# A hybrid decoder block on one core: seven Strassen gate pairs instead of six, operand sums from a stored x, early products in turn, and LayerNorm written behind the third pair

## The chip, the cores and the metric

The kernel runs on one core of one Trainium2 chip. The metric is the device time of one execution in microseconds (us); three executions of the kernel before gave 1420.69, 1419.81 and 1416.16 us, median 1419.81 us. The engines are named as in the profile: PE (TensorE), DVE (VectorE), ACT (ScalarE), POOL (GpSimd) and SP (SyncE, which here only issues DMAs). Each engine works through its own instructions in the order in which the compiled program has them.

## The reference, cut to what matters

One layer, sequence 1024, width 1024, everything float32:

```python
mod = silu(c) @ ada_w + ada_b
sh1, sc1, ga1, sh2, sc2, ga2 = split(mod, 6)
h = rmsnorm(x, pre_mix_g) * (1 + sc1) + sh1
glu_in, qkv, gates = split(h @ w_in, [1024, 2560])       # gates: 2 x 1024 columns
u = silu(layernorm(causal_depthwise_conv(glu(glu_in))))  # 512 channels
y_conv = u @ w_conv_out                                  # 512 -> 1024
y_att = stick_breaking_attention(qkv) @ w_att_out        # 512 -> 1024
g_conv, g_att = split(gates, 2)
y = (sigmoid(g_conv) * y_conv + sigmoid(g_att) * y_att) @ w_o
x = x + ga1 * rmsnorm(y, post_mix_g)
# then a SwiGLU sub-layer of the same build
```

The change concerns the product for `gates`, a 1024 x 2048 weight times h, the LayerNorm of the convolution branch, and the two stages behind them, `u @ w_conv_out` and `o @ w_att_out`.

## The kernel before, in words

Activations lie transposed: h is eight tiles of 128 channels x 1024 positions. Each float32 operand is split into two parts of the fp32r type, hi and lo (`hhi[k]`, `hlo[k]`), and a product takes three matmuls: hi by hi, hi by lo, lo by hi. A matmul instruction is 128x128 weights by 512 positions, into one bank of PSUM.

The stages stand in this order: the first RMSNorm and projections; attention, GLU and convolution; the gates; LayerNorm; `y_conv` (L772); `y_att` (L801 on); the product by w_o; the SwiGLU sub-layer. The order of instructions on each engine is made by a scheduler from the program order, the priorities in the code and the moment at which it thinks that data and buffers are free, so that pieces of later stages stand between earlier ones. A ring is a set of buffers with one tag: the n-th tile takes the buffer of the (n - bufs)-th and waits until that one's last reader is done.

**Gates.** The 16 row blocks of the gate matrix form eight pairs. `NPL` = 2 pairs (four blocks `n`) are plain products (L611-615, bank `pg`): 24 matmuls for each half of the positions, 192 in all. The other six pairs are 2x2 block products by a seven-product scheme of Strassen's kind: 7 products of 12 matmuls instead of 8. Two products of a pair, with the unchanged operands B11 (`hhi[0..3]`, `hlo[0..3]`) and B21 (`hhi[4..7]`, `hlo[4..7]`), are the early ones (L617-628): each has its own bank (`k1`, `k2`), the first is copied to `ee0` and stored to DRAM (`e_d0`), the second is added to it on DVE. 144 matmuls in all. The other five (`other_five`, L697-712) use the banks `ka` and `kc` and weight sums `s1`..`s4`: 360 matmuls in all. Their data operands T1..T4 are sums of blocks of h, formed once (L660-670): `f` is a ring of two tiles of 128x1024, filled on DVE with hi + lo, four subtractions follow for each `j`, and `make_t` splits each sum in hi (ACT) and lo (DVE).

**LayerNorm.** `ln_all` (L722-759) loads the convolution's result (`cr0`..`cr3`) and works in two halves of 512 positions: sums over channels by a matmul with ones (`lnm`, `lnv`), subtraction, squares, reciprocal root, then swish into `csil`, from which `chi` and `clo` are split. It is written behind the first pair (`LN_AT` = 0) with a raised priority (`LN_PRI` = 100). Its tiles come from the ring `hp` (tag `act`, 16 buffers), whose first 16 tiles are hhi and hlo, in turn.

**The two products behind.** `y_conv(n)` (L772-783) is 24 matmuls for each of eight `n`, into `pyc`; weights `wc0, 2, 4, 6` come through `load_w` by the ring `wraw` (three buffers of 128x1024 in the pool `wp`). Behind each `y_conv` stand two dots on DVE (`ada2_dots`, L764), by which the modulation of the second sub-layer is formed; their weights `ada2_16..31` come through the ring `f` (two buffers). Then `of0`..`of3` (the attention output, ring `wraw`) are split into `ohi`, `olo`, and `y_att` needs those and `wa0, 2, 4, 6` (ring `wraw` too) for `pya`.

Loads are issued by SP, one after another; an issue that waits for a buffer holds up those behind it. Stores to the DRAM tiles of the gates are issued by POOL.

Of the kernel before, what the change touches and what calls it, by code (L numbers as in the profile page):

```python
# [47 lines left out]
LN_AT = 0  # L48
SOONER = 5000
EARLY = 11  # L50
TLATER = 40
# [22 lines left out]
def tile_block(ctx: ExitStack, tc: tile.TileContext, xT, vecs, ada1, ada2, win, wv, wcv, wat, wo, w1, w2, cvw, out):  # L74
# [15 lines left out]
    cb_d = dp.tile([P, D], F32, name="cb_d")  # L90
    s_d = [dp.tile([P, T], F32, name=f"s_d{n}") for n in range(2 * KT)]
    e_d0 = [dp.tile([P, CH], F32, name=f"e_d0_{i}") for i in range(KT)]
    g_d = [dp.tile([P, 2, 2, CH], F32, name=f"g_d{k}") for k in range(FH)]
    w_d = [dp.tile([P, 4, 2, CH], F32, name=f"w_d{k}") for k in range(FH)]

# [5 lines left out]
    def load(dst, src):  # L101
        return nc.sync.dma_start(dst, src)
# [100 lines left out]
    with ExitStack() as s0:  # L203
# [146 lines left out]
        for k in range(KT):  # L350
            kn = k + 1
            if kn < KT:
                if kn not in SH_DVE:
                    shift_act(kn)
                if kn + 1 < KT and kn + 1 not in SH_DVE:
                    shift_pe(kn + 1)
                x_op(kn)
                if kn <= 2:
                    w0_hi(kn)
                hi_op(kn)  # L360
                if kn + 1 < KT:
                    dots(kn + 1)
                if kn <= 2:
                    w0_lo(kn)
            if k:
                lo_op(k)
            ws = (q0b, k0b, gg0b)
            if k <= 1:
                for i in range(k + 1):
                    gemm_k(ws[i], w0s[i], k)  # L370
                for kk in range(k + 1):
                    gemm_k(ws[k + 1], w0s[k + 1], kk)
            else:
                for b_, w_ in zip(ws, w0s):
                    gemm_k(b_, w_, k)
# [34 lines left out]
    with ExitStack() as sC:  # L410
        pc = mkpool(sC, "pc")
        with ExitStack() as sA:
# [196 lines left out]
            for n in PLAIN:  # L609
                gb = banks2(f"pg{n}")  # L610
                gemm(gb, load_w(win[20 + n], f"wg{n}"), h, range(KT))  # L611
                for c in range(NCH):
                    sg = sgp.tile([P, CH], F32, tag="sg", name=f"sg{n}_{c}", bufs=2)
                    act.activation(sg, gb[c], AF.Sigmoid, bias=0.0, scale=1.0)
                    store(s_d[n][:, c * CH:(c + 1) * CH], sg)
            for i in GPAIRS:
                raw = wp.tile([P, T], F32, tag="wraw", name=f"ew{i}")  # L617
                load(raw, win[20 + 2 * i])
# [3 lines left out]
                act.activation(e[0], k1, AF.Copy)  # L622
                store(e_d0[i], e[0])
# [3 lines left out]
                act.activation(e[1], e[1], AF.Sigmoid, bias=0.0, scale=1.0)  # L627
                store(s_d[2 * i][:, :CH], e[1])

    sV.close()  # L630
    with ExitStack() as sG:
# [22 lines left out]
        def make_t(name, src, hi_eng, lo_eng):  # L654
# [2 lines left out]
            lo_eng.tensor_tensor(t[:, 1], src, t[:, 0], op=ALU.subtract)  # L657
            return t

        for j in range(HK):  # L660
# [3 lines left out]
            b11, b12, b21, b22 = f[0][:, :CH], f[0][:, CH:], f[1][:, :CH], f[1][:, CH:]  # L664
            dve.tensor_tensor(b11, b12, b11, op=ALU.subtract)
            dve.tensor_tensor(b12, b22, b12, op=ALU.subtract)
            dve.tensor_tensor(b22, b22, b11, op=ALU.subtract)
            dve.tensor_tensor(b21, b21, b22, op=ALU.subtract)
            for b, src in (("T2", b22), ("T3", b12), ("T1", b11), ("T4", b21)):
                B0[b, j] = make_t(f"{b}o_{j}", src, act, dve)  # L670

        pairs, p1s = {}, {}
# [13 lines left out]

        def other_five(i):
            wg, wu = pairs[i]
            p1 = p1s[i]
            a11, a12, a21, a22 = wg[:, :CH], wg[:, CH:], wu[:, :CH], wu[:, CH:]  # L690
            s1, s2, s3 = (st(f"g{nm}_{i}") for nm in ("s1", "s2", "s3"))
            v, w_, c21 = xt(f"gv_{i}"), xt(f"gw_{i}"), xt(f"gc_{i}")
            dve.tensor_tensor(s1, a21, a22, op=ALU.add)
            dve.tensor_tensor(s2, s1, a11, op=ALU.subtract)
            s2o = w_op(f"s2o_{i}", s2, act, GP)
# [15 lines left out]
            dve.tensor_tensor(c21, ka, p1, op=ALU.add)  # L711
            sig_out(c21, 2 * i + 1, 0)

        cacc, chi, clo, yc, wcs = [], [], [], [], {}

        def split_r(src, names, hi_eng, lo_eng):
            hi, lo = (hp.tile([P, T], F32R, tag="act", name=nm) for nm in names)
# [1 line left out]
            lo_eng.tensor_tensor(lo, src, hi, op=ALU.subtract)  # L719
            return hi, lo  # L720

        def ln_all():  # L722
            for ct in range(CONVT):
                t = hp.tile([P, T], F32, tag="act", name=f"cr{ct}")
                load(t, channels(u_d[ct]))
                cacc.append(t)
            for c in range(NCH):
                cs = slice(c * CH, (c + 1) * CH)
                la, lm, ls = (hp.tile([P, 2, CH], F32, tag="act", name=f"l{nm}{c}") for nm in "ams")
                s0_, s1_, mean = la[:, 0], la[:, 1], lm[:, 0]  # L730
                e0 = dve if c in LN_DVE0 else pool
                e0.tensor_tensor(s0_, cacc[0][:, cs], cacc[1][:, cs], op=ALU.add)
                for ct in (2, 3):
                    e0.tensor_tensor(s0_, s0_, cacc[ct][:, cs], op=ALU.add)
                pm = psg.tile([P, CH], F32, tag="ln", name=f"lnm{c}", bufs=1)
                pe.matmul(pm, ones, s0_, start=True, stop=True)
                act.activation(mean, pm, AF.Copy, bias=0.0, scale=1.0 / 512)
                for ct in range(CONVT):
                    dve.tensor_tensor(cacc[ct][:, cs], cacc[ct][:, cs], mean, op=ALU.subtract)
                    if ct == 0:  # L740
                        act.activation(s1_, cacc[ct][:, cs], AF.Square)
                    else:
                        act.activation(ls[:, ct % 2], cacc[ct][:, cs], AF.Square)
                        (dve if c in LN_DVE1 else pool).tensor_tensor(s1_, s1_, ls[:, ct % 2], op=ALU.add)
                pvv = psg.tile([P, CH], F32, tag="ln", name=f"lnv{c}", bufs=1)
                pe.matmul(pvv, ones, s1_, start=True, stop=True)
                rstd_from(s0_, lm[:, 1], s1_, pvv, 512)
                for ct in range(CONVT):
                    dve.tensor_tensor(cacc[ct][:, cs], cacc[ct][:, cs], s0_, op=ALU.mult)
            for ct in range(CONVT):  # L750
                a = cacc[ct]
                g, b_ = vec[:, C_LNG + ct:C_LNG + ct + 1], vec[:, C_LNB + ct:C_LNB + ct + 1]
                sg = hp.tile([P, T], F32, tag="act", name=f"csig{ct}")
                act.activation(sg, a, AF.Sigmoid, bias=b_, scale=g)
                act.activation(a, a, AF.Identity, bias=b_, scale=g)
                o = hp.tile([P, T], F32, tag="act", name=f"csil{ct}")
                ar, sr = (t.rearrange("p (r m) -> p r m", r=PH) for t in (a, sg))
                (pool if ct in SILU_POOL else dve).tensor_tensor(
                    o.rearrange("p (m r) -> p r m", r=PH), ar, sr, op=ALU.mult)
                cacc[ct] = o  # L760

        a2 = deque(range(2 * KT, 4 * KT))

        def ada2_dots(ins, n):  # L764
            for _ in range(n):
                col = a2.popleft()
                w = pg.tile([P, D], F32, tag="f", name=f"ada2_{col}", bufs=2)
                load(w, ada2[col - 2 * KT])
                with tc.issue_after(ins.ins):
                    dot_c(w, cb, col)  # L770

        def y_conv(n):  # L772
# [5 lines left out]
            gemm(yb, wcs[n // 2], (chi, clo), range(4), woff=(n % 2) * CH)  # L778
            for c in range(NCH):
                cs = slice(c * CH, (c + 1) * CH)  # L780
                last = dve.tensor_tensor(y[:, cs], yb[c], y[:, cs], op=ALU.mult)
# [11 lines left out]
        for ct in range(CONVT):  # L793
            hi, lo = split_r(cacc[ct], (f"chi{ct}", f"clo{ct}"), act, dve)
            chi.append(hi)
            clo.append(lo)
        for n in range(KT):
            ada2_dots(y_conv(n), 2)
        ohi, olo = [], []
# [989 lines left out]
```

## Time and profile before

| | |
|---|---|
| median of three executions | 1419.81 us (1416.16 to 1420.69) |
| profiled execution | 1416.97 us; its span in the trace 1415.2 us, mean granted clock 0.991 |
| PE busy | 1378.3 us, 97% |
| DVE busy | 1059.9 us, 75% |
| ACT busy | 652.7 us, 46% |
| POOL busy | 102.0 us, 7% |
| first matmul of the other five products | 477.25 us |
| last early product ends | 485.41 us |
| first matmul of y_conv / of y_att | 571.52 us / 620.49 us |

Times in the trace count from the start of the span; the profiled execution takes 1.8 us more than its span. PE is the engine that is nearly always busy: the length of the kernel is PE's work plus the moments in which PE has nothing that it may start. So the places to look at are PE's gaps, and for a changed order the question is at which places PE's next instruction is not ready.

### The profile page before, as it was taken

The numbers are of one execution on the slowest core, as the hardware profiler recorded it, in microseconds if no ns is written. First come the engines' busy times: TensorE is split into PE (matmuls) and PEld (weight loads), VectorE is DVE, ScalarE is ACT, GpSimd is POOL, SyncE is SP. The second block draws the span as 40 slices with busy tenths as digits, with TensorE's granted clock in tenths as the row PEclk, the third lists the DMA queues.
The fourth block names the chain that finished last, engine by engine and source line by source line (L and its number), as shares of the span: only waits on it lengthen the run. The fifth ranks groups of instructions, "written<-read, shape, count | busy, mean of one in ns | idle before, by whom it ended". The sixth has DMA issues, their size and how long they took to land.

```text
span 1415.2 us, 18817 instructions
## 1 busy us (share of the span) xinstructions
PE 1378.3 (97%) x6822; PEld 1157.6 (82%) x6822; DVE 1059.9 (75%) x1602; ACT 652.7 (46%) x1136; POOL 102.0 (7%) x245
## 2 busy tenths in 40 slices
PE   7999999999999999999999999999999999999996
PEld 4798898998888877787877778888878887888886
DVE  6898687575857788877579878688877776785357
ACT  5375466364554457312356553234434444334441
POOL 0000000000001111000012100001111110000000
PEclk8999999999999999999999999999999999999998
DMA  9212040140453746764935545456777769597833
GB/s 383 74 36 90 16 164 30 46 150 31 122 162 119 260 149 224 281 209 131 345 119 170 182 147 178 157 172 225 247 250 251 259 241 391 172 334 280 281 116 119
DMA packets 91116, 258.72 MB, mean 183 GB/s; under 512 B 9744, under 2 KB 20112, under 8 KB 90000
## 3 DMA queue, kind: packets, MB, share of 16 engines
q1 hardware_dynamic: 75088, 202.99, 42.4%
q0 software_dynamic: 15936, 54.54, 10.4%
q8 instruction: 53, 0.87, 0.2%
q14 instruction: 39, 0.32, 0.1%
HBM read 190.91 MB, written 66.58 MB: 182 GB/s over the span
## 4 chain that ended last, share of the span: by engine, by line
PE 76%; DVE 8%; DMA 6%; issue 5%; ACT 3%; POOL 1%; SPq 0%; DVEq 0%; POOLq 0%; ACTq 0%
PE ka L956 12%; PE ka L1498 8%; PE kc L956 7%; PE pwo L879 6%; PE pb L1498 4%; PE pgv L172 3%; PE pg L172 3%; PE pv L476 3%; PE pcv L456 3%; PE tr L569 2%; PE pgg L172 2%; PE pk L172 2%; PE pq L172 2%; PE k L407 2%; PE pa L1498 2%
## 5 line engine op out<-in xcount | busy, mean ns | idle before, releaser
L548 ACT ACTIVATE ka<-z 128x128 f32<-128x128 f32 (+2 forms) x96 | 47.0, 496 | 54.1 <-PE z L547 49.6
L573 DVE TENSOR_TENSOR alo<-tr,ahi 128x512 fp32r<-128x512 f32 x80 | 53.4, 685 | 21.4 <-ACT ahi L572 20.7
L554 DVE TENSOR_TENSOR_SCAN ka<-ka,eye 128x128 f32<-128x128 f32 (+1 forms) x64 | 52.1, 831 | 21.8 <-ACT ka L548 21.7
L572 ACT ACTIVATE ahi<-tr 128x512 fp32r<-128x512 f32 x80 | 46.7, 603 | 39.1 <-PE av L578 22.9
L1498 PE MATMUL ka<-gt,w2f 128*128 128x512 f32 x264 | 63.5, 390 | 0.2 <-DMA w2f<-w_d 0.2
L559 DVE TENSOR_TENSOR be<-be,ka 128x127 f32<-128x127 f32 (+2 forms) x96 | 51.2, 551 | 11.9 <-ACT be L550 8.5
L1498 PEld LDWEIGHTS ka<-gt,w2f 128*128 128x128 f32 x264 | 49.4, 188 | 11.2 <-issue 1.0
L1064 PE MATMUL ke<-b,w_hi 128*128 128x512 f32 x176 | 55.1, 394 | 0.0
L550 ACT ACTIVATE be<-z 128x127 f32<-128x127 f32 (+2 forms) x96 | 46.5, 497 | 18.4 <-PE tr L569 18.2
L127 DVE SCALAR_TENSOR_TENSOR ada<-ada,cb 128x1024 f32<-128x1024 f32 x32 | 38.8, 1223 | 19.8 <-DMA ada<-in_ada_dram 19.7
L569 PE MATMUL tr<-ident,be 128*128 128x128 f32 x288 | 46.6, 272 | 0.0
L557 DVE TENSOR_TENSOR_SCAN ka<-ka 128x512 f32<-128x512 f32 x32 | 40.4, 1274 | 6.3 <-ACT ka L548 6.3
L578 PE MATMUL av<-ahi,vst 128*128 128x256 f32 x160 | 43.9, 292 | 0.0
L456 PE MATMUL pcv<-ph,cvw 128*128 128x128 f32 x320 | 42.1, 275 | 1.8 <-DMA ph<-v_d 1.8
L579 PE MATMUL av<-alo,vst 128*128 128x256 f32 x160 | 42.2, 290 | 0.0
L456 PEld LDWEIGHTS pcv<-ph,cvw 128*128 128x128 f32 x320 | 39.8, 191 | 2.7 <-issue 1.9
L1064 PEld LDWEIGHTS ke<-b,w_hi 128*128 128x128 f32 x176 | 33.0, 188 | 7.8 <-issue 1.0
L476 PE MATMUL pv<-wv_hi,hhi 128*128 128x256 f32 x128 | 36.6, 286 | 2.3 <-DVE qst L500 1.4
L151 ACT ACTIVATE gt<-X 128x512 fp32r<-128x512 f32 x33 | 20.4, 630 | 39.3 <-PE ka L1498 12.3
L879 PE MATMUL pwo<-mhi,wo_hi 128*128 128x512 f32 x88 | 34.7, 395 | 2.0 <-DVE sga L819 2.0
L476 PE MATMUL pv<-wv_lo,hhi 128*128 128x256 f32 x128 | 36.3, 285 | 0.0
L476 PE MATMUL pv<-wv_hi,hlo 128*128 128x256 f32 x128 | 36.3, 284 | 0.0
(531 smaller groups left out, 4113.5 us busy)
## 6 DMA issues: line engine op xcount, KB each, us to landing
w_d<-w2o POOLq DMA_DIRECT2D x44, 512.0 KB, 7.7
w2f<-w_d SPq DMA_DIRECT2D x44, 512.0 KB, 5.0
ada<-in_ada_dram SPq DMA_DIRECT2D x32, 512.0 KB, 5.4
w2r<-in_w_dram SPq DMA_DIRECT2D x44, 256.0 KB, 3.8
w1g<-in_w_dram SPq DMA_DIRECT2D x21, 512.0 KB, 3.7
w1u<-in_w_dram SPq DMA_DIRECT2D x21, 512.0 KB, 5.4
cvw<-in_cvw_dram SPq DMA_DIRECT2D x20, 512.0 KB, 3.7
ada_w<-in_ada_dram SPq DMA_DIRECT2D x8, 1024.0 KB, 12.0
```

Of the source, the lines that this page charges most:

```text
L172: pe.matmul(bank, st[:, cols], mv[k][:, c * CH:(c + 1) * CH], start=(i == 0 and s == 0), stop=(i == n - 1 and s == 2))
L456: pe.matmul(cv[:, gi * TM:(gi + 1) * TM], wts[n][:, at:at + P], ph[:, g, SH - 1 - d:SH - 1 - d + TM], start=(d == 0), stop=(d == SH - 1))
L476: pe.matmul(pv[:, :256], st[k][:, tcols], mv[:, wc], start=(k == 0 and i == 0), stop=(k == KT - 1 and i == 2))
L548: act.activation(kap[:, s_lo:s_hi], z[:, zo:zo + w], AF.Sigmoid, bias=0.0, scale=-0.125)
L554: dve.tensor_tensor_scan(rev, rev, eye[:, CH - w:][:, ::-1], 0.0, op0=ALU.mult, op1=ALU.add)
L559: dve.tensor_tensor(beta[:, :m], beta[:, :m], kap[:, s_lo + 1:s_lo + 1 + m], op=ALU.mult)
L569: pe.transpose(tr[:, o:o + P], src, ident)
L573: dve.tensor_tensor(alo, tr, ahi, op=ALU.subtract)
L879: pe.matmul(bank_, st[:, cols], mv[k][:, cs], start=(k == 0 and q == 0), stop=(k == KT - 1 and q == 2))
L956: pe.matmul(bank_, st[:, cols], t[:, mv], start=(first and j == 0 and s == 0), stop=(j == HK - 1 and s == 2), skip_group_check=not first)
L1064: pe.matmul(kbs[f], wes[f][st][:, cols], t[:, mv], start=(i == 0 and j == 0 and q == 0), stop=(j == HK - 1 and q == 2), skip_group_check=i ...
L1498: pe.matmul(dst, w[st][:, cols], g[mv], start=first and s == 0, stop=last and s == 2, skip_group_check=more)
```

## The change

- `NPL` 2 -> 1: one plain pair, seven Strassen pairs. PE has 96 plain matmuls fewer, 24 early ones and 60 of the other five more: 12 fewer.
- The early products go in turn: the first of pair i+1 stands ahead of the second of pair i. Both products of a pair accumulate in one bank `k`, so that DVE's addition goes (six additions); the tiles `ee` get a ring of three.
- In the first stage, each `x` (x times its norm and scale, without the shift) is stored to a new DRAM tile `xm_d[k]`, eight stores of 512 KB on POOL's queue. The sums for T1..T4 are formed from 16 loads of 256 KB of it, on SP's queue, instead of hi + lo; the shift is added by scalar operands. For j = 0 they go to the ring `f`, for j = 1 and 3 to the ring `x` (seven tiles), for j = 2 to the ring `s` (four tiles, the ring of the weight sums `s1`..`s3`). Eight DVE additions of 128x1024 go.
- `ln_all` is written behind the third pair (`LN_AT` = 2) without a raised priority, with fewer tiles: `cr0`..`cr3` take the buffers of hhi0, hlo0, hhi1, hlo1, `la` and `lm` those of hhi2, hlo2; `chi` and `clo` lie in the first halves of hhi4..7 and hlo4..7 and in tiles `cb`, two of which are in the ring `f`.
- The weights of the dots, `ada2_16..31`, move from the ring `f` to the ring `wraw`, with the `wc`, `of` and `wa` loads.
- `c21` takes the place of `p1` and needs no tile of its own.

```diff
-NPL = 2
+NPL = 1
...
-LN_PRI = 100
-LN_DVE0 = (0, 1)
-LN_DVE1 = (0, 1)
-SILU_POOL = ()
-LN_AT = 0
+LN_AT = 2
...
+            store(xm_d[k], xs[k])
...
-            for i in GPAIRS:
...
-                e = [sgp.tile([P, CH], F32, tag="sg", name=f"ee{q}_{i}", bufs=2) for q in range(2)]
-                k1 = bank(f"k1_{i}")
-                prod0(k1, w_op(f"a11_{i}", raw[:, :CH], act, dve), "B11")
...
-                k2 = bank(f"k2_{i}")
-                prod0(k2, w_op(f"a12_{i}", raw[:, CH:], act, dve), "B21")
-                dve.tensor_tensor(e[1], k2, e[0], op=ALU.add)
...
+            def early(i, q):
...
+                k, raw = kes[i]
+                w = w_op(f"a1{q + 1}_{i}", raw[:, q * CH:(q + 1) * CH], act, dve)
+                prod0(k, w, ("B11", "B21")[q], q == 0)
+                e = pc.tile([P, CH], F32, tag="ee", name=f"ee{q}_{i}", bufs=3)
+                act.activation(e, k, (AF.Copy, AF.Sigmoid)[q])
...
+            for n, i in enumerate(GPAIRS):
+                early(i, 0)
+                if n:
+                    early(GPAIRS[n - 1], 1)
+            early(GPAIRS[-1], 1)
...
         for j in range(HK):
-            f = [pg.tile([P, T], F32, tag="f", name=f"f{q}_{j}", bufs=2) for q in range(2)]
-            dve.tensor_tensor(f[0], hhi[j], hlo[j], op=ALU.add)
-            dve.tensor_tensor(f[1], hhi[HK + j], hlo[HK + j], op=ALU.add)
...
+            if j == 0:
...
+            else:
+                b12, b11, b22, b21 = ((xt, st, xt)[j - 1](f"f{q}_{j}") for q in range(4))
+            for b, k, c in ((b12, j, 1), (b11, j, 0), (b22, HK + j, 1), (b21, HK + j, 0)):
+                load(b, xm_d[k][:, c * CH:(c + 1) * CH])
+            sh, ds = mod[:, HK + j:HK + j + 1], dsh1[:, j:j + 1]
             dve.tensor_tensor(b11, b12, b11, op=ALU.subtract)
-            dve.tensor_tensor(b12, b22, b12, op=ALU.subtract)
...
+            dve.scalar_tensor_tensor(b12, b22, ds, b12, op0=ALU.add, op1=ALU.subtract)
...
         def ln_all():
+            cr = [hp.tile([P, T], F32, tag="act", name=f"cr{ct}") for ct in range(CONVT)]
             for ct in range(CONVT):
-                t = hp.tile([P, T], F32, tag="act", name=f"cr{ct}")
-                load(t, channels(u_d[ct]))
...
+                load(cr[ct], channels(u_d[ct]))
+            la, lm = (hp.tile([P, 2, CH], F32, tag="act", name=f"l{nm}") for nm in "am")
...
-                w = pg.tile([P, D], F32, tag="f", name=f"ada2_{col}", bufs=2)
+                w = wp.tile([P, D], F32, tag="wraw", name=f"ada2_{col}")
                 load(w, ada2[col - 2 * KT])
...
             if q == LN_AT:
-                with tc.high_priority(offset=LN_PRI):
-                    ln_all()
+                ln_all()
```

What the scheduler makes of it shows in the order of instructions at three places.

On DVE before, behind the last rows of attention (`oT3`) and the first early weights (`a12_0`), the sums for T begin:

```order
L394 TENSOR_TENSOR a12_0_4438<-ew0_4415,a12_0_4438 128x512
L583 TENSOR_TENSOR oT3_3602<-av3_1_1_4017,oT3_3602 64x512
L662 TENSOR_TENSOR f0_0_4672<-hhi0_269,hlo0_270 128x1024
L663 TENSOR_TENSOR f1_0_4673<-hhi4_277,hlo4_278 128x1024
L665 TENSOR_TENSOR f0_0_4672<-f0_0_4672 128x512
L666 TENSOR_TENSOR f0_0_4672<-f1_0_4673,f0_0_4672 128x512
```

On DVE now, these rows stand behind the last split of the last early weights (`a12_6`, pair 6), with LayerNorm's first half ahead of the sums:

```order
L392 TENSOR_TENSOR a12_6_4562<-ew6_4523,a12_6_4562 128x512
L748 TENSOR_TENSOR la_5010<-cr0_5002,cr1_5003 128x512
L750 TENSOR_TENSOR la_5010<-la_5010,cr2_5004 128x512
L750 TENSOR_TENSOR la_5010<-la_5010,cr3_5005 128x512
L756 TENSOR_TENSOR cr0_5002<-cr0_5002,lm_5011 128x512
L756 TENSOR_TENSOR cr1_5003<-cr1_5003,lm_5011 128x512
L756 TENSOR_TENSOR cr2_5004<-cr2_5004,lm_5011 128x512
L756 TENSOR_TENSOR cr3_5005<-cr3_5005,lm_5011 128x512
L760 TENSOR_TENSOR la_5010<-la_5010,lm_5011 128x512
L675 TENSOR_TENSOR f0_0_4593<-f0_0_4593 128x512
```

The sums began in the middle of the early weights and now begin behind all of them and behind LayerNorm's first rows. From the first row of `la` there are 47 DVE rows up to the first weight sum of pair 0, `gs1_0`, which stands here (T1o_3 is T1 of j = 3):

```order
L661 TENSOR_TENSOR T2o_3_4675<-f2_3_4665,T2o_3_4675 128x512
L661 TENSOR_TENSOR T1o_3_4678<-f1_3_4664,T1o_3_4678 128x512
L703 TENSOR_TENSOR gs1_0_4699<-gw0b_4689 128x512
L661 TENSOR_TENSOR T3o_3_4681<-f0_3_4663,T3o_3_4681 128x512
L748 TENSOR_TENSOR la_5010<-cr0_5002,cr1_5003 128x512
```

In the order of before, `gs1_0` stood directly behind the last early weights, `a12_5`, and ahead of the last sums.

On PE before, the end of the early products (`k2_4`, `k1_5`) has a product of pair 0 (`ka_0`) between them:

```order
L407 MATMUL k2_4_4601<-hhi7_283,a12_4_4602 128x512
L407 MATMUL ka_0_4777<-T2o_0_4680,s2o_0_4772 128x512 x3
L407 MATMUL ka_0_4777<-T2o_1_4700,s2o_0_4772 128x512 x3
L407 MATMUL ka_0_4777<-T2o_2_4720,s2o_0_4772 128x512 x3
L407 MATMUL ka_0_4777<-T2o_3_4740,s2o_0_4772 128x512 x3
L407 MATMUL k1_5_4624<-hhi0_269,a11_5_4625 128x512
```

On PE now, behind the last early product there are two rows of LayerNorm, and then the pairs, beginning with `s1o_0`, which is split from `gs1_0`:

```order
L405 MATMUL k_6_4525<-hhi7_291,a12_6_4562 128x512
L752 MATMUL lnm0_5015<-la_5010,ones_148 128x512
L762 MATMUL lnv0_5029<-la_5010,ones_148 128x512
L405 MATMUL kc_0_4712<-T1o_0_4606,s1o_0_4726 128x512 x2
L405 MATMUL ka_0_4711<-T2o_0_4603,s2o_0_4706 128x512 x2
L405 MATMUL kc_0_4712<-T1o_0_4606,s1o_0_4726 128x512
```

The product of pair 0 that stood among the early ones has gone behind all of them, and the two rows of LayerNorm have come ahead of it.

On SP before, the loads of `of` and `wa` at the end of y_conv stand among loads of `ada2`, each in its own ring:

```order
L102 DMA of3_5812<-o_d3_77 128x1024
L102 DMA sga3_0_5944<-s_d11_98 128x512
L102 DMA wa0_raw_5818<-in_wat_dram 128x1024
L102 DMA wa2_raw_5900<-in_wat_dram 128x1024
L102 DMA ada2_20_5596<-in_ada2_dram 128x1024
L102 DMA ada2_21_5599<-in_ada2_dram 128x1024
```

On SP now, all are in the one ring of three buffers:

```order
L99 DMA wc6_raw_5740<-in_wcv_dram 128x1024
L99 DMA ada2_28_5776<-in_ada2_dram 128x1024
L99 DMA ada2_29_5779<-in_ada2_dram 128x1024
L99 DMA ada2_30_5812<-in_ada2_dram 128x1024
L99 DMA ada2_31_5815<-in_ada2_dram 128x1024
L99 DMA of0_5818<-o_d0_74 128x1024
L99 DMA of1_5824<-o_d1_75 128x1024
L99 DMA of2_5830<-o_d2_76 128x1024
L99 DMA of3_5836<-o_d3_77 128x1024
L99 DMA wa0_raw_5842<-in_wat_dram 128x1024
```

The full order of that ring is wc0, ada2_16 to 19, wc2, 20 to 23, wc4, 24 to 27, wc6, 28 to 31, of0 to 3, wa0, 2, 4, 6. Each load now waits for the last reader of the third one ahead of it, and for an `ada2` that is a dot behind a `y_conv`; in this order `y_att`'s first weights stand behind all the dots.

More of the change, by code (lines that the diff above doesn't have):

```diff
@@ L92, in tile_block @@
     e_d0 = [dp.tile([P, CH], F32, name=f"e_d0_{i}") for i in range(KT)]
+    xm_d = [dp.tile([P, T], F32, name=f"xm_d{k}") for k in range(KT)]
     g_d = [dp.tile([P, 2, 2, CH], F32, name=f"g_d{k}") for k in range(FH)]
@@ L720, in split_r, with gemm_halves @@
             return hi, lo
+        def gemm_halves(banks, w, a, woff):
+            for i in range(CONVT):
+                cols = slice(woff + i * P, woff + (i + 1) * P)
+                for s, (st_, mv) in enumerate(((0, 0), (0, 1), (1, 0))):
+                    for c, bank_ in banks.items():
+                        pe.matmul(bank_, w[st_][:, cols], a[mv][i][c], start=(i == 0 and s == 0),
+                                  stop=(i == CONVT - 1 and s == 2))
         def ln_all():
+            cr = [hp.tile([P, T], F32, tag="act", name=f"cr{ct}") for ct in range(CONVT)]
             for ct in range(CONVT):
-                t = hp.tile([P, T], F32, tag="act", name=f"cr{ct}")
-                load(t, channels(u_d[ct]))
-                cacc.append(t)
+                load(cr[ct], channels(u_d[ct]))
+            la, lm = (hp.tile([P, 2, CH], F32, tag="act", name=f"l{nm}") for nm in "am")
+            s0_, s1_, mean, sq = la[:, 0], la[:, 1], lm[:, 0], lm[:, 1]
             for c in range(NCH):
[L728 to L732, printed above, removed]
+                cs = hs[c]
+                dve.tensor_tensor(s0_, cr[0][:, cs], cr[1][:, cs], op=ALU.add)
                 for ct in (2, 3):
-                    e0.tensor_tensor(s0_, s0_, cacc[ct][:, cs], op=ALU.add)
+                    dve.tensor_tensor(s0_, s0_, cr[ct][:, cs], op=ALU.add)
                 pm = psg.tile([P, CH], F32, tag="ln", name=f"lnm{c}", bufs=1)
@@ L738, in ln_all @@
                 for ct in range(CONVT):
[L739 to L744, printed above, removed]
+                    t = cr[ct][:, cs]
@@ L745, in ln_all @@
+                    dve.tensor_tensor(t, t, mean, op=ALU.subtract)
+                    q = (s1_, sq, s0_, sq)[ct]
+                    act.activation(q, t, AF.Square)
+                    if ct:
+                        dve.tensor_tensor(s1_, s1_, q, op=ALU.add)
                 pvv = psg.tile([P, CH], F32, tag="ln", name=f"lnv{c}", bufs=1)
                 pe.matmul(pvv, ones, s1_, start=True, stop=True)
-                rstd_from(s0_, lm[:, 1], s1_, pvv, 512)
+                rstd_from(s0_, mean, s1_, pvv, 512)
```

56 lines of the change are left out of this document (31 added, 25 removed).

## The prediction

> **What bounds the kernel now.** The page of the profile comes first: its busy times and its chain of work that ended last.
>
> ```profile
> PE 1378.3 (97%) x6822; PEld 1157.6 (82%) x6822; DVE 1059.9 (75%) x1602; ACT 652.7 (46%) x1136; POOL 102.0 (7%) x245
> PE 76%; DVE 8%; DMA 6%; issue 5%; ACT 3%; POOL 1%; SPq 0%; DVEq 0%; POOLq 0%; ACTq 0%
> ```
>
> PE is busy for 97%, and three quarters of the chain are PE's. An engine beside it matters where PE has to wait for it. So I went from the page to the stages that the change touches, by the table of windows (stretch, its length, then busy time and instructions of PE, PEld, DVE, ACT, POOL; granted PE clock, DMA share, GB/s).
>
> ```profile
> 450.00:477.00 27.00, 27.00 (x120) 22.34 (x120) 26.02 (x40) 17.30 (x32) 5.06 (x10) 1.00 0.54 185
> 477.00:571.00 94.00, 89.24 (x368) 70.69 (x367) 80.13 (x120) 53.57 (x76) 10.56 (x20) 0.96 0.62 219
> 571.00:620.30 49.30, 49.30 (x219) 40.79 (x219) 37.13 (x52) 12.00 (x14) 1.62 (x3) 1.00 0.74 260
> 525.00:550.00 25.00, 22.81 (x90) 17.49 (x89) 21.31 (x36) 12.66 (x19) 2.16 (x4) 0.93 0.43 140
> 550.00:571.00 21.00, 18.43 (x74) 14.52 (x73) 20.86 (x25) 18.17 (x22) 2.69 (x5) 0.92 0.87 322
> ```
>
> The early products (first row) and y_conv (third) leave PE no gap. Among the pairs (second) PE loses a little, and DVE is busy for 85%. In the first row DVE is busy for 26.02 of 27.00 us: there it forms the T sums, hidden under early products. PE's waits in the second stretch are few:
>
> ```profile
> PE ka L407 <- DVE gv L701: 2.3, 1, 2.3
> PE kc L407 <- ACT s1o L151: 2.1, 1, 2.1
> PE ka L407 <- DVE gw L705: 0.2, 1, 0.2
> ```
>
> The timeline of PE gives the price of a matmul, the end of the early products and the start of y_att:
>
> ```profile
> 485.41 1.29 PE L407 MATMUL ka<-T3o,s3o 128*128 128x512 f32 x5
> 486.54 2.88 PE L407 MATMUL kc<-T1o,s1o 128*128 128x512 f32 x12
> 489.26 1.75 PE L407 MATMUL ka<-T3o,s3o 128*128 128x512 f32 x7
> 531.95 0.73 PE L407 MATMUL kc<-T1o,s1o 128*128 128x512 f32 x2 [2.13 <-ACT s1o L151]
> 620.49 0.62 PE L172 MATMUL pya<-ohi,wa_hi 128*128 128x512 f32 x2
> ```
>
> Twelve matmuls take 489.26 - 486.54 = 2.72 us, 0.2267 each. The 368 of the second stretch would take 83.4; 10.6 us are lost there.
>
> **The change part by part.**
>
> *Fewer matmuls.* 96 plain ones go, 24 early and 60 of the other five come: 12 fewer, 2.7 us. This is certain and on PE's path.
>
> *The end of the early products.* Up to the last one PE has 96 fewer plain, 24 more early, and the 12 of ka_0 now stand behind: 84 fewer, 19.0 us. The end comes at 485.41 - 19.0 = 466.4, if nothing holds the early ones up; DVE's six additions there go, and their weights were split in time before.
>
> *What PE finds next.* By the order it is lnm0, lnv0 and s1o_0. So pair 0 cannot begin before DVE has come through the 47 rows ahead of gs1_0, the first of which needs `cr0`, `cr1`. Their buffers are hhi0 and hlo0, which the first product of pair 6 reads; its start is 36 matmuls before the end, and 33 of them come after the third, which is the last reader of both: 466.4 - 7.5 = 458.9 at the earliest. SP's 16 loads for the sums are queued behind those four, so the sums cannot come first either. The rows for DMA and DVE:
>
> ```profile
> 480.61 3.32 SPq L102 DMA_DIRECT2D cr<-u_d  x4
> 490.52 0.69 DVE L732 TENSOR_TENSOR la<-cr,cr 128x512 f32<-128x512 f32 x1 [2.83 <-DMA cr<-u_d]
> 491.98 0.69 DVE L734 TENSOR_TENSOR la<-la,cr 128x512 f32<-128x512 f32 x1 [0.77 <-DMA cr<-u_d]
> 525.21 2.49 DVE L749 TENSOR_TENSOR cr<-cr,la 128x512 f32<-128x512 f32 x4
> 527.62 0.69 DVE L694 TENSOR_TENSOR gs<-gs,gw4a 128x512 f32<-128x512 f32 x1
> L737 ACT ACTIVATE lm<-lnm x2: 579/589/599, 497.1 to 522.8; 128x512 f32<-128x512 f32 x2
> L736 PE MATMUL lnm<-la,ones x4: 590/592/595, 496.1 to 521.2; 128*128 128x512 f32 x4
> ```
>
> In the trace `cr` took 9.9 us from issue to use (480.61 to 490.52), with DMA busy. Loads of the same size land in 4.5 (the `of` loads, below). I take 6, since few loads stand ahead: first `la` at 464.9. A row costs (527.62 - 525.21)/4 = 0.60 us, so 48 rows with gs1_0 take 29.0. Within them DVE waits for the mean: lnm (two matmuls, at most 1.2 by the last row) and ACT's 0.59 lie between the third row and the fourth, so with the way between the engines 2.2; and for `cr2`, `cr3` 1.5 (two gaps like the 0.77). gs1_0 is done at 464.9 + 29.0 + 2.2 + 1.5 = 497.6, its hi on ACT some 0.6 later: **498.2**. PE has nothing for 498.2 - 466.4 = **31.8 us** but two small sums. Lower bound: `cr` lands in 4.5 and nothing waits on the way, 26; upper: `cr` takes the 9.9 and DVE waits 2 to 3 us more for ACT, 38. In before DVE did the sums while PE had early products; that cover is gone.
>
> *The five products of seven pairs.* 420 matmuls, 95.2 us, and LayerNorm's second half on PE, at most 4 x 0.59 = 2.4. Lost before: 10.6. Now one pair more shares DVE, but most T sums and half of LayerNorm are done by then; pair 1's second load `gw1b` waits for pair 0's sums and is needed soon after. I take 12, bounds 7 and 18.
>
> *y_conv in one ring.* Behind two dots each, `wc2`, `wc4` and `wc6` are loaded too late, and at the end `of1` waits for the dot of `ada2_30` and `wa0` for the split of `of1`.
>
> ```profile
> L102 SPq DMA_DIRECT2D of<-o_d x4: 319/320/327, 573.7 to 588.3; - x4
> L151 ACT ACTIVATE ohi<-of x4: 1041/1061/1062, 576.9 to 593.8; 128x1024 fp32r<-128x1024 f32 x4
> L805 DVE TENSOR_TENSOR olo<-of,ohi x4: 1217/1219/1227, 578.0 to 595.1; 128x1024 fp32r<-128x1024 f32 x4
> DMA to landing us min/median/max: 3.2/4.5/6.2
> ...
> DMA to landing us min/median/max: 3.5/4.8/5.3
> ...
> 583.51 1.29 DVE L781 TENSOR_TENSOR yc<-pyc,yc 128x512 f32<-128x512 f32 x2 [1.12 <-PE pyc L172]
> 584.72 1.22 DVE L127 SCALAR_TENSOR_TENSOR ada<-ada,cb 128x1024 f32<-128x1024 f32 x1
> 585.86 0.08 DVE L127 DVE_READ_ACCUMULATOR ada<-ada,cb 128x1 f32 x1
> ```
>
> (The first landing line is that of `of`, the second of `wa`.) A y_conv is 24 matmuls, 5.4 us. From the end of y_conv(0) it takes 1.3 for its two multiplications, 2.3 for two dots (1.14 from start to start), 4.5 for the load of `wc2`, 1.1 for its hi: 9.2, and y_conv(1) covers 5.4. That is 3.8 of waiting, three times: 11.4, or 11.9 with a little for the lo. At the end nothing covers: 1.3 + 1.1 (dot 30) + 4.5 (`of1`) + 1.1 + 1.2 (its hi and lo) + 4.8 (`wa0`) + 1.1 = 15.1. Together **27**. With loads of 3.5 it is 22, with 5.4 to 6.2 it is 32.
>
> The Trainium skill, page "DMA: Bandwidth & Descriptors", section "Anatomy of one DMA", gives about 2.0 us fixed plus the bytes at 436 GB/s, which for 512 KB is an estimate of 3.2; the stops would then be 21 and the forecast 6 earlier. The median rows of 4.5 and 4.8 here, with the other loads beside them, are longer, and I go by them.
>
> *The clock behind a wait.* After the wait of 2.13 us the stretch from 525 to 550 has clock 0.93, that from 550 to 571 has 0.92: 0.07 x 25 or 0.08 x 21, 1.7 us each. Five long waits (one of 32, three of 4, one of 15): 8.5; in the shorter ones among the pairs it is in the 10.6 already. Since the three of 4 may not all do it, I take 6, bounds 3 and 9.
>
> The Trainium skill, page "TensorE: Matmul & The Clock Gate", Part 1, states half rate after an idle window of about 3.4 us until the engine has been busy for as long. By it a wait of 2.13 need not have lowered the clock, which the trace shows that it did; the sum by the rule would hold 1.7 for each of five, 8.5.
>
> *The start.* The eight stores of x add 4 MB while DMA is full, and the first stage's DVE has little slack:
>
> ```profile
> 20.00:30.00 10.00, 7.33 (x47) 6.84 (x46) 9.61 (x14) 5.16 (x9) 0.00 (x0) 0.71 1.03 424
> 30.00:40.00 10.00, 10.00 (x50) 8.56 (x49) 9.93 (x13) 4.34 (x6) 0.00 (x0) 0.78 1.01 413
> L102 SPq DMA_DIRECT2D ada_w<-in_ada_dram x8: 327/328/483, 5.2 to 31.8; - x8
> ```
>
> About three of them (1.5 MB) fall into these 20 us, 3.6 us of DMA at 413 GB/s; the loads that they meet, `ada_w`, are the ones issued by 31.8. DVE does not wait there (busy 9.6 and 9.9 of 10), so I take 0, upper bound 3.7; no gain, since nothing leaves. On POOL they stand ahead of fills that attention needs at 50 us, when the x are long formed.
>
> *At nothing:* c21 in p1's tile, the single bank `k`, and DVE's 8 + 6 additions less, since DVE is not what PE waits for once the order is as shown.
>
> **Sum.** y_att begins at 498.2 + 612 x 0.2267 (420 and y_conv's 192: 138.7) + 2.4 + 12 + 27 + 6 = 684.3, before 620.5: **+63.8 us**. All behind it is as before. The profiled execution took 1416.97, so 1481; the median of the runs shown, 1419.81, is 0.2% above it, which the range covers. The terms' bounds: below -6 -5 -5 -3, above +6 +6 +5 +3 (and 3.7 of the start), not all at once: 1464 to 1500.
>
> **The rivals.**
>
> 1. *Only the first wait.* The ring hides its loads, because DVE's dots come sooner behind y_conv or LayerNorm's end delays y_conv while loads run ahead. For it: in before no `wa` or `of` load held up PE. Against: the order of the ring. 1481 - 27 - 4 x 1.7 of the clock, less what is then late: about 1449.
> 2. *Only the ring.* The T sums end by the time that early products do; then -2.7 + 27 + some 7 of clock: 1448, or 1437 if the 10.6 among the pairs go too. Against: cr0's buffer is free at 458.9 at the earliest.
> 3. *Faster.* Neither wait: the buffers of h come free and DVE, with 14 additions less and six pairs' sums done early, keeps ahead, so PE never waits among the pairs. 1417 - 2.7 - 10.6 = 1404. It decides at gs1_0: it must be formed by 466, 32 us sooner than I have it.
> 4. *No change* but the 12 matmuls: 1414, within 0.3%, which is about what a measurement of this kernel can tell.
> 5. *More.* LayerNorm's first half waits for ACT row by row, and with both T hi and squares on ACT the sums take half as long again (48 rows, +15), or the start is held up too: 1501 to 1510.
>
> **How the numbers follow.** Forecast 0.74, rival 1 0.10, rival 2 0.05, rival 3 0.04, rival 4 0.02, rival 5 0.05. The range 1444 to 1501 holds the forecast's own (which I trust for nine in ten of its cases) and rivals 1 and most of 2. Faster 0.04, same 0.02, slower 0.94.
>
> **What would show it.** After 466 us a PE gap of some 30 us ahead of the first kc, its releaser ACT s1o or DVE; the first `la` at 465 behind DMA `cr`; the T sums from about 470 to 500 on DVE; y_conv with four waits for wc_hi and wa_hi (ACT), the last about 15 us; y_att from 684. It is wrong if PE's first kc follows the last early product within 10 us, or if y_conv runs its 192 matmuls in under 50 us.

## The result, and the profile after

The changed kernel takes 1474.61 us (median of four, 1473.31 to 1475.95) against 1418.95 before: ratio 1.0394, 95% interval 1.0373 to 1.0416. It is 55.7 us slower; 1481, or 64 more, was forecast. The first lines of its page:

```profile
span 1471.7 us, 18882 instructions
PE 1385.5 (94%) x6810; PEld 1160.5 (79%) x6810; DVE 1055.8 (72%) x1607; ACT 657.0 (45%) x1146; POOL 107.2 (7%) x254
```

PE has fallen from 97% to 94% of a longer span. Those of its waits that are new say where (total in us, times, longest):

```profile
PE kc L405 <- ACT s1o L148: 20.9, 1, 20.9
PE pya L169 <- ACT wa_hi L148: 13.5, 1, 13.5
PE pyc L737 <- ACT wc_hi L148: 12.5, 3, 4.5
PE lnv L762 <- DVE la L760: 6.3, 1, 6.3
...
PE lnm L752 <- DVE la L750: 2.4, 1, 2.4
```

None of the five is in the list of before. Three belong to one gap, which the timeline of PE shows: from the end of the last early product (467.08 + 0.39) to the first pair it does only the two small sums of LayerNorm.

```profile
467.08 0.39 PE L405 MATMUL k<-hhi,a 128*128 128x512 f32 x1
469.92 1.10 PE L752 MATMUL lnm<-la,ones 128*128 128x512 f32 x2 [2.45 <-DVE la L750]
477.30 2.07 PE L762 MATMUL lnv<-la,ones 128*128 128x512 f32 x2 [6.29 <-DVE la L760]
500.31 1.22 PE L405 MATMUL kc<-T1o,s1o 128*128 128x512 f32 x2 [20.93 <-ACT s1o L148]
502.71 1.22 PE L405 MATMUL ka<-T2o,s2o 128*128 128x512 f32 x2 [1.19 <-ACT s2o L148]
503.73 4.47 PE L405 MATMUL kc<-T1o,s1o 128*128 128x512 f32 x10
508.00 2.67 PE L405 MATMUL ka<-T2o,s2o 128*128 128x512 f32 x10
```

In the same time, SP's timeline (taken up to 480 us, with 15 of the 16 loads for the sums) has those loads (`f`) behind the ones of `cr`:

```profile
459.80 1.75 SPq L99 DMA_DIRECT2D cr<-u_d  x4
461.59 14.03 SPq L99 DMA_DIRECT2D f<-xm_d  x15
```

And DVE's timeline has 12.4 us of waiting ahead of the first `la`; from there DVE works through to `gs`, but for three waits of 1.2, 1.1 and 1.9 us:

```profile
465.48 0.69 DVE L748 TENSOR_TENSOR la<-cr,cr 128x512 f32<-128x512 f32 x1 [12.40 <-DMA cr<-u_d]
...
498.91 0.68 DVE L703 TENSOR_TENSOR gs<-gw0b 128x512 f32<-128x512 f32 x1
```

The other two are for the weights of y_conv and of y_att (`wc_hi`, `wa_hi`), which come through the ring `wraw`; y_att begins at 678.3 instead of 620.5.

### The profile page after: what moved, and what is told of

It is laid out like the page before. It is cut to its first block, busy times and chain, and to the rows that moved or that the text cites. A ratio compares the mean times of both kernels' runs of the same rounds, so it can differ in the third digit from the quotient of the medians.

```text
span 1471.7 us, 18882 instructions
## 1 busy us (share of the span) xinstructions
PE 1385.5 (94%) x6810; PEld 1160.5 (79%) x6810; DVE 1055.8 (72%) x1607; ACT 657.0 (45%) x1146; POOL 107.2 (7%) x254
## 4 chain that ended last, share of the span: by engine, by line
PE 82%; DVE 7%; issue 4%; DMA 4%; ACT 2%; POOL 1%; DVEq 0%; SPq 0%; ACTq 0%; POOLq 0%
PE ka L974 13%; PE ka L1516 8%; PE kc L974 7%; PE pwo L897 6%; PE pb L1516 4%; PE pya L169 3%; PE pgv L169 3%; PE pv L474 3%; PE ka L405 2%; PE tr L567 2%; PE pyc L737 2%; PE pgg L169 2%; PE pk L169 2%; PE pq L169 2%; PE pcv L454 2%
## 5 line engine op out<-in xcount | busy, mean ns | idle before, releaser
L124 DVE SCALAR_TENSOR_TENSOR ada<-ada,cb 128x1024 f32<-128x1024 f32 x32 | 38.4, 1220 | 10.7 <-DMA ada<-in_ada_dram 10.6
L405 PE MATMUL kc<-T1o,s1o 128*128 128x512 f32 x84 | 24.5, 425 | 20.9 <-ACT s1o L148 20.9
L405 PEld LDWEIGHTS kc<-T1o,s1o 128*128 128x128 f32 x84 | 17.3, 208 | 26.3 <-ACT s1o L148 22.5
```

The source lines that it names most:

```text
L405: pe.matmul(bank_, w[st][:, cols], mvs[mv], start=(first and j == 0 and s == 0), stop=(j == HK - 1 and s == 2), skip_group_check=not first)
```

## The experiments

Two edits take the two waits away, alone and together. Times are medians; each ratio is to the kernel before, run beside it.

**e1: the dots' weights out of the ring.** LayerNorm's tiles `la` and `lm` are free when y_conv begins, so the loads go there:

```diff
+            lnt.extend((la, lm))
...
-                w = wp.tile([P, D], F32, tag="wraw", name=f"ada2_{col}")
+                w = flat(lnt[col % 2])
```

> The changed kernel, with the weights of the 16 dots loaded into la and lm, LayerNorm's two tiles that are free by then, instead of the ring wraw that wc, of and wa share. Theory (the ring's waits are real and independent of the first wait): y_conv's stretch, 77.5 us from 600.8 to 678.3 in the changed kernel, falls to 45-52 us, the gap of 33 us ahead of the first kc stays; 1474.6 - 28 = about 1446 us (1441 to 1452). Rival (y_conv is late because of DVE's dots or of DMA bandwidth, not of the buffers): over 1465 us, with PE still waiting for wc_hi and wa_hi.

Measured: 1444.36 us, ratio 1.0191 (1.0172 to 1.021), as the theory expected. The first gap is as it was, and wc_hi and wa_hi are gone from PE's waits, of which these are the first two:

```profile
PE kc L405 <- ACT s1o L148: 20.9, 1, 20.9
PE lnv L763 <- DVE la L761: 6.3, 1, 6.3
```

y_conv runs from 603.1 to 649.4, 46.3 us instead of 77.5, by the rows of its matmuls and y_att's (the two times are the first and the last start):

```profile
L737 PE MATMUL pyc<-hhi,wc_hi x32: 389/389/389, 603.1 to 648.0; 128*128 128x512 f32 x32
L169 PE MATMUL pya<-ohi,wa_hi x64: 389/389/389, 649.4 to 691.7; 128*128 128x512 f32 x64
```

Both stretches hold 204 matmuls, y_conv's 192 and the last pair's last 12, which at 0.2267 take 46.2. So the ring's buffers were the cause of the second wait, not DVE's dots, which are the same, nor the DMAs, which move the same bytes: 31.2 us (77.5 - 46.3), of which 26.0 are waits and some 5 what each stop costs behind it, slow matmuls above all.

**e2: one pool for ee.** The prediction took the order as given. Why DVE's sums stood so late was open, and LayerNorm's new place was the first suspect. Another was a detail of the diff: `ee` moved from the pool `sgp` to `pc`, which must be closed before `pg`, the pool of the sums, can open.

```diff
-                e = pc.tile([P, CH], F32, tag="ee", name=f"ee{q}_{i}", bufs=3)
+                e = sgp.tile([P, CH], F32, tag="sg", name=f"ee{q}_{i}", bufs=2)
```

> The changed kernel, with the tiles ee of the early products put back in the ring sg (two buffers, as before) instead of the pool pc; nothing else. Theory M (the T sums start late because their tiles lie on the memory of ee and cannot be loaded before the last early product is copied and stored): T sums start near 440 us, the gap of 33 us ahead of the first kc goes, 1474.6 - 33 - 3 of clock = about 1438 us, up to 1448 if the pairs then wait for DVE as before (10 us). Rival L (LayerNorm's place in the program and its loads ahead on SP make the wait): the gap stays, 1470 to 1476 us.

Measured: 1450.94 us, ratio 1.0231 (1.0212 to 1.025). With `ee` back, LayerNorm's rows are behind the sums again (the first `la` runs at 472.82), though `ln_all` stands where the change put it. The first sum runs on DVE at 441.19 instead of 474.70:

```profile
441.19 0.69 DVE L675 TENSOR_TENSOR f<-f 128x512 f32<-128x512 f32 x1 [0.69 <-DMA f<-xm_d]
```

And pair 0 begins on PE among the early products, at 471.80 instead of 502.71 for T2o:

```profile
471.80 0.61 PE L405 MATMUL ka<-T2o,s2o 128*128 128x512 f32 x2
```

The gap of 33 us is gone; rival L is out. A smaller wait has come, the third in PE's list: the ring `sg` has two buffers, and the banks `k` wait for ACT's copies to `ee`, which wait until the stores of the ones before have read them (ACT waits 4.1 us for `e_d` and 3.4 for `s_d`).

```profile
PE pyc L737 <- ACT wc_hi L148: 14.3, 3, 5.0
PE pya L169 <- ACT wa_hi L148: 13.4, 1, 13.4
PE k L405 <- ACT ee L625: 5.5, 5, 2.5
```

So the third buffer of `ee` had a use, in the wrong pool. The wait is the largest part of what is missing to 1438, not all of it: by the profiled executions e2 takes 27.0 us (1471.7 - 1444.7) where 36 were expected, 5.5 of the 9 are this wait, and the ring's two waits have grown by 1.7. The median, 1450.94, lies 4.5 above the profiled execution, and no trace shows that part.

**e3: both edits, and e11, the same again.**

> The edits of the two runs before together. Theory (two separate waits, which add): 1474.6 - 28 - 36 = about 1410 us, up to 1418 if the pairs wait for DVE. If one wait only moves to the other's place, over 1430 us. Against the kernel before (1419) the 12 matmuls less are 2.7 us, so between 1406 and 1418 the rest of the change is worth between +10 and -1 us.

> The kernel of e3 again, in more rounds and beside the two others. It was 0.9964 of the kernel before (0.994 to 0.9987); if that holds: a ratio between 0.994 and 0.998, about 1412 to 1415 us, so that the changed kernel without its two waits is faster than the kernel before by more than the 0.2% of its 12 matmuls. If not: 0.998 to 1.000.

Measured: e3 1412.85 us, ratio 0.9964 (0.994 to 0.9987); e11, in twice as many executions, 1414.49 and 0.9971 (0.9954 to 0.9987). From the changed kernel's median e1 takes 30.3 us, e2 23.7 and both 61.8; from the span of its profiled execution, 1471.7, they take 31.8, 27.0 and 61.9. So the two waits are separate, and neither moves to the other's place; that both edits together take some 3 to 8 us more than the two alone is not explained. Without the waits the change is a gain of 0.3%, as both intervals end below 1; that it is more than the 0.2% of the 12 matmuls is not shown. What PE still waits for most in e3 is `ee`:

```profile
PE k L405 <- ACT ee L625: 4.5, 3, 2.6
```

and y_att's matmuls begin at 618.1, 2.4 us ahead of the kernel before, but at 620.5 in e11, which is the same kernel:

```profile
L169 PE MATMUL pya<-ohi,wa_hi x64: 389/389/389, 618.1 to 660.5; 128*128 128x512 f32 x64
```

Behind that point both take 791.7 us (1409.8 - 618.1, 1412.2 - 620.5), and the kernel before 794.7 (1415.2 - 620.5), with a wait of 2.0 for `sga` that the two do not have. So in e11's profiled execution the whole gain lies behind y_att, not in the gates; that fewer matmuls there made it is not shown.

**e5: the same pool in the kernel before.** If the pool alone makes the first wait, it must do so without anything else of the change.

```diff
-                e = [sgp.tile([P, CH], F32, tag="sg", name=f"ee{q}_{i}", bufs=2) for q in range(2)]
+                e = [pc.tile([P, CH], F32, tag="ee", name=f"ee{q}_{i}", bufs=3) for q in range(2)]
```

> The kernel before with one edit: its tiles ee in the pool pc with three buffers, as in the changed kernel. Theory M (that pool's memory lies under the tiles of the T sums): the sums start only after the last early products, near 480 us instead of 431, and PE waits 10 to 30 us ahead of the pairs; 1430 to 1450 us. Rival L (the wait came with LayerNorm's place and the loads from DRAM, of which this kernel has nothing): 1417 to 1421 us.

Measured: 1453.75 us, ratio 1.022 (1.0192 to 1.0247): this one line, which like the changed kernel also gives `ee` three buffers, costs the kernel before some 31 us by the ratio, a little more than Theory M's range. The sums start at 486.72 on DVE instead of 431.60:

```profile
486.72 1.22 DVE L662 TENSOR_TENSOR f<-hhi,hlo 128x1024 f32<-128x1024 f32 x1
```

and at the head of PE's waits stand T2o and LayerNorm's sum:

```profile
PE ka L407 <- ACT T2o L151: 18.0, 3, 8.6
PE lnm L736 <- DVE la L734: 6.0, 1, 6.0
PE ka L407 <- ACT s2o L151: 5.1, 2, 4.3
```

With e2 this settles that the pool makes the wait. One step is less sure: my expectation said that the sums' tiles lie on ee's memory. In the compiled program's addresses only two of the 16 T tiles do (T3 and T4 of j = 1); the tiles of j = 0 went behind too. Nor did the first loads wait for `ee` when the changed kernel ran: they were issued from 461.59 on, and the last early product ended at 467.47. What was late is their place in the order, behind `cr`. So the scheduler seems to hold back the whole pool when it makes the order. That is read from the program; no run here tells it apart.

**e4 and e9: seven pairs alone, then with the early products.** e4 is the kernel before with `NPL = 1`.

> The kernel before with one plain pair and seven Strassen pairs, nothing else. Theory (12 matmuls of 0.2267 us are 2.7 us, all on PE's path): 1416 us (1413 to 1418). Rival (DVE, at 85% among the pairs, becomes the bound there with seven pairs): 1422 us or more.

Measured: 1425.57 us, ratio 1.0059 (1.0038 to 1.0079): 12 matmuls fewer, and 7 us slower, as the rival expected. PE's waits where the pairs begin are above all for the T sums of DVE and ACT, LayerNorm's sum and the additions to `gw` and `ee`:

```profile
PE ka L407 <- ACT T2o L151: 3.4, 1, 3.4
PE lnm L736 <- DVE la L734: 2.8, 1, 2.8
PE ka L407 <- DVE gw L705: 2.0, 1, 2.0
PE kc L407 <- DVE ee L626: 1.9, 1, 1.9
PE ka L407 <- DVE T2o L657: 1.1, 1, 1.1
PE kc L407 <- DVE T1o L657: 1.1, 1, 1.1
```

e9 adds the changed kernel's early products (in turn, both in one bank, the loop of the front part's diff) with `ee` left in `sg`.

> The kernel of e4 (before with seven pairs, 1425.6 us) with the early products as in the changed kernel, in turn and both in one bank, so that DVE's seven additions of 0.6 us go; their tiles stay in the ring sg. If DVE's load while the T sums are formed is what cost e4 its 7 us: 1416 to 1420 us, and PE's waits for T2o, T1o and ee (8 us in e4) fall by half or more. If not: 1424 to 1427.

Measured: 1418.34 us, ratio 1.0004 (0.9988 to 1.0021). The seven us are back, and the waits for T fall to 0.8, though others for `s2o`, 6.6 together, have come:

```profile
PE ka L407 <- ACT s2o L151: 3.8, 2, 3.0
PE ka L407 <- DVE s2o L394: 2.8, 1, 2.8
PE ka L407 <- DVE T2o L663: 0.5, 1, 0.5
PE ka L407 <- ACT T2o L151: 0.3, 1, 0.3
```

The two runs fit the theory that DVE's load there decides, but e9 changes bank and turn with the additions, and does not part them. The traces add a limit: y_att begins at 631.2 in e4 and at 626.2 in e9, both later than the 620.5 of before, and behind it they take 791.5 and 790.5 instead of 794.7. So e9 brings back five of the 10.7 us that e4 loses ahead of y_att, and most of the rest is made up behind it.

**e6, e7: single parts taken from e3.** e6 forms the sums from hi + lo again, as before, and drops the stores of x:

```diff
+            f = [pg.tile([P, T], F32, tag="f", name=f"f{q}_{j}", bufs=2) for q in range(2)]
+            dve.tensor_tensor(f[0], hhi[j], hlo[j], op=ALU.add)
...
-            store(xm_d[k], xs[k])
```

> The kernel of e3 (both waits taken away, 1412.9 us) with the T sums formed from hi + lo on DVE, as before, and without the stores of x. If the sums from DRAM are what lets DVE keep up with seven pairs: 1418 to 1425 us, as in the run with seven pairs alone (1425.6), with PE waiting for T. If they are worth nothing: 1411 to 1414.

e7 puts a pair's two early products one behind the other:

```diff
-            for n, i in enumerate(GPAIRS):
-                early(i, 0)
-                if n:
-                    early(GPAIRS[n - 1], 1)
-            early(GPAIRS[-1], 1)
+            for i in GPAIRS:
+                early(i, 0)
+                early(i, 1)
```

> The kernel of e3 with the two early products of a pair one behind the other, not in turn with the next pair's. If the turns only spare waits for the weights' splits, PE waits for a12 some 1 us in each of seven pairs: 1415 to 1420 us. If they do nothing (or cost, by the bank that is held longer): 1408 to 1413.

Measured: e6 1416.12 us, ratio 0.9977 (0.9957 to 0.9998); e7 1417.18, 0.9968 (0.9952 to 0.9985). Neither is told from e3 (0.9964). Both of e6's expectations missed: it is not as slow as 1418, and PE has waits for s2o and s1o again (8.2 us with LayerNorm's sum), but no longer those for `ee`. e7's time lies in the first of its ranges, but beside a kernel before of 1420.17, and PE's list has no wait for a12; it has 3.6 for s2o and 5.1 for `ee`. So no worth of the sums from DRAM or of the turns is shown in the time; the intervals leave room for some 0.4% of each.

**e8, e10: a third buffer for ee, elsewhere.** The first early product of a pair is copied into the half of the raw weight tile that has been read: for all pairs in e8, for pairs 1, 2 and 3 in e10.

```diff
-                e = sgp.tile([P, CH], F32, tag="sg", name=f"ee{q}_{i}", bufs=2)
+                e = sgp.tile([P, CH], F32, tag="sg", name=f"ee{q}_{i}", bufs=2) if q or i not in (1, 2, 3) else raw[:, :CH]
```

> The kernel of e3 with the first early product of each pair copied into the half of the raw weight tile that is read already, so that the ring sg's two buffers serve the second products alone. Theory (the 4.5 us that PE waits for ACT's ee in e3 are waits for a buffer of that ring): 1408 to 1410 us. If the raw tiles, held longer, delay the next weights or pair 0's: 1413 to 1425.

> The kernel of e3 with the first early product copied into the raw weight tile for pairs 1, 2 and 3 only, so that the last weights and pair 0's are not held up as in e8. If the 4.5 us of waits for ee in e3 go without a new wait: 1408 to 1411 us. If pair 0's weights are late again: 1414 to 1422.

Measured: e8 1423.88 us, ratio 1.0033 (1.001 to 1.0057): the raw tiles are held longer, pair 0's second load (`gw0b`) is issued at 476.52 instead of e3's 451.68, and PE waits for s1o (4.7). e10 1409.85, ratio 0.9953 (0.9935 to 0.997), the lowest of all here; its interval overlaps that of e3, so a lead over e3 is not shown. What the trace shows is that the waits for `ee`, 4.5 in e3, are nearly gone; PE's waits at the gates are now:

```profile
PE k L405 <- ACT a L148: 1.5, 2, 1.1
PE ka L405 <- DVE gv L711: 1.0, 1, 1.0
PE k L405 <- ACT ee L625: 0.3, 1, 0.3
PE kc L405 <- ACT ee L625: 0.2, 1, 0.2
```

## Why the prediction was right, point by point

- *End of the early products*: 466.4 forecast, 467.5 measured.
- *The first gap*: first `la` at 464.9, measured 465.48; gs1_0 done at 497.6, measured 499.6; first pair at 498.2, measured 500.31. The gap was to be 31.8 and is 33. The order of the engines with one DVE row at 0.60 us gave it; six us for `cr` were about right (459.80 to 465.48). What the prediction did not see is the reason behind the order: it spoke of LayerNorm's rows as what stood ahead, and they are there because of the pool in which `ee` had been put (e2, e5).
- *The pairs*: this term was mis-sized, and lies outside its own bounds. 12 us, at least 7, were to be lost. Between 500.31 and y_conv's first matmul at 600.8 lie 100.5 us; with the last 12 matmuls of the pairs, which stand behind that one, it is 103.2, where 95.2 + 2.4 + 12 = 109.6 were forecast. So 5.6 were lost, and 2.8 of them belong to the clock (below): 2.8 instead of 12. PE waited 2.1 (1.19, 0.59 and 0.32). The prediction named the reason, that most T sums and half of LayerNorm are done by then, and took too little of it. The gap is not needed for it: in e2, e3 and e11, which have none, PE waits only 0.9 among the pairs. With the sums formed on DVE from hi + lo (e6) it is 8.2.
- *y_conv in one ring*: 27 forecast, 12.5 + 13.5 = 26.0 measured. It is the chain that the prediction described; the first three waits were a little longer than the 11.9 forecast and the last shorter than 15.1, so that the errors partly cancel (`wa0` is issued at 672.66, when the lo of `of1`, begun at 671.40, is done). The loads landed in 4.3 (`of`, median), 4.4 (`wc`) and 4.5 (`wa`), near the 4.5 and 4.8 of before. By the Trainium skill's fit ("DMA: Bandwidth & Descriptors", "Anatomy of one DMA"), which that section gives for DMAs issued by GpSimd and not by SP as here, the estimate is 3.2 and the sum 21 (worked out again, 20); the medians do not agree with it, and only the fastest load of `of`, 3.2, does.
- *The clock behind a wait*: 6 for all, bounds 3 and 9. The fourteen matmuls from 500.31 to 508.00 ran at about half rate (ten take 508.00 - 503.73 = 4.27 us, 0.43 each), 14 x 0.2 = 2.8 more; behind the three stops within y_conv it is the 31.2 of e1 less 26.0, 5.2. Together 8. The loss behind the last stop the prediction put ahead of y_att too, but it falls behind y_att's first matmul: ten matmuls take 682.66 - 678.31 = 4.35 us instead of 2.27, 2.1 more. One reading behind this term was loose: the low clock of 550 to 571 in the kernel before lies behind the wait of 2.3 for `gv`, not behind the one of 2.13.
- *The start*: 0 forecast. The trace shows the stores as DMA traffic that goes on longer (315 GB/s between 40 and 50 us, 36 before), and DVE as busy as it was; the first matmul of attention's scores (`z<-kst`) begins at 78.6, and at 78.8 before. The window in the changed kernel, with DVE's busy time behind PE's and PEld's, and the same in the kernel before:

```profile
40.00:50.00 10.00, 10.00 (x48) 8.32 (x48) 9.86 (x17) 2.83 (x4) 1.06 (x2) 1.00 0.77 315
```

```profile
40.00:50.00 10.00, 10.00 (x49) 8.36 (x50) 9.86 (x17) 3.02 (x4) 0.00 (x0) 1.00 0.09 36
```

- *The sum*: y_att at 684.3, measured 678.3. Forecast too long were the pairs by 9 us and y_conv's waits by 1, too short the start of the pairs by 2 and the clock ahead of y_att by 2. So the two long waits were right in mechanism and size; that the total is off by only six owes something to luck, as the errors partly cancel. Behind y_att the kernel is 1.3 us shorter (1471.7 - 678.3 against 1415.2 - 620.5), where "as before" was forecast: it loses the 2.1 of the clock there, and the wait of 2.0 for `sga` in the stage by w_o is gone.
- *The rivals*: each of rivals 1 and 2 was the time with one wait alone. Measured: 1444 with only the first (e1; 1449 forecast), 1451 with only the ring (e2; 1448 forecast). Rival 3 with neither was 1404; e3 and e11 give 1413 to 1414, with 4.5 to 4.8 of waits for `ee` in their place, and e10, nearly without these, gives 1410. The rest of the difference is not accounted for. Worked out again, rival 1's sum gives 1447 instead of 1449, and rival 5's 15 us more give 1496, or 1500 with the start held up too, instead of 1501 to 1510.

## What to carry to other kernels

The scheduler here seems to have held back a whole pool for the last tile of the pool ahead of it; one scratch ring in the wrong pool cost some 31 us (e5). So a scratch tile belongs in a pool that lives past the stage which should overlap; where an order looks strange, look at what had to be released before it. A ring shared by loads of two users makes each wait for the slower user's reads: before merging rings, write the sequence down and ask of every load whose reader three places ahead it waits for. Fewer instructions on the busiest engine bring their time only if its feeder keeps up: 12 matmuls less made 7 us more (e4) until the early products were rearranged too (e9), which took additions off DVE among other things. And where a gain is small, look in the trace for the stage in which it arises: e11's lies behind the stages that were changed.

## What the runs showed of the hardware that I had not expected

How long matmuls run at half rate behind a wait was not one fixed stretch. Behind the gap, with 20.9 us of idle time at its end, they took 0.43 us instead of 0.2267 from 500.31 to 508.00 (granted clock 0.50 there), with a stop of 1.19 within. Behind the first wait for `wc_hi`, of 3.63, it was 618.24 to 621.27. Behind the 13.5 of y_att's first wait it was 678.31 to 682.66:

```profile
678.31 1.22 PE L169 MATMUL pya<-ohi,wa_hi 128*128 128x512 f32 x2 [13.53 <-ACT wa_hi L148]
679.33 1.05 PE L169 MATMUL pya<-olo,wa_hi 128*128 128x512 f32 x2
...
682.66 0.62 PE L169 MATMUL pya<-ohi,wa_hi 128*128 128x512 f32 x2
```

The Trainium skill, "TensorE: Matmul & The Clock Gate", Part 1, gives half rate until some 3.4 us of busy work; the 4.35 us of the last case are somewhat longer, the 7.7 of the first twice that, with a stop of a third of such a window in it.

A wait of some 2.5 us lowered the clock in one execution and not in another. In e3 a wait of 2.59 is followed by some 1.5 us at full rate, then by half rate up to about 463.2 (two matmuls in 0.85 us), then by full rate again:

```profile
458.29 0.50 PE L405 MATMUL k<-hhi,a 128*128 128x512 f32 x1 [2.59 <-ACT ee L625]
...
460.60 1.05 PE L405 MATMUL k<-hhi,a 128*128 128x512 f32 x2
...
464.59 0.62 PE L405 MATMUL k<-hhi,a 128*128 128x512 f32 x2
```

In e11, the same kernel, the same wait is followed by 0.8 us at full rate and then by half rate up to about 465.0. In e2 a wait of 2.54 ends at 459.74, and no slow matmul follows: two of them take 461.48 - 461.03 = 0.45 us, and so it goes on. So the length of a wait alone does not tell the slow stretch behind it; what does was not tested here.
